# Seven block products in place of eight in the down product of a feed-forward block, each between two up tiles of the next group

## The chip, the cores and the metric

The kernel runs on one core of a Trainium2 chip. The metric is device microseconds of one execution, the median of several runs. The engines are TensorE (PE, matmuls; PEld are its weight loads), VectorE (DVE), ScalarE (ACT), GpSimd (POOL) and SyncE (SP, which here only issues DMAs).

## The reference, cut to what matters

One layer of a decoder: RMS norm, one projection, attention heads beside mLSTM heads, an output projection, and then a feed-forward block. The change touches only the last two lines of it.

```python
D_MODEL = 1024
SEQ = 512
D_FF = 4 * D_MODEL
...
    x = x + rms_norm(mixed @ w_out, g_mix_post)

    u = rms_norm(x, g_mlp_pre) @ w_up
    u = jnp.square(jax.nn.relu(u))
    x = x + rms_norm(u @ w_down, g_mlp_post)
    return x
```

Everything is float32. `u` is 512 tokens by 4096 features, `w_down` is 4096 by 1024.

## The kernel before

**Precision.** A float32 operand is split in two tiles of the matmul type fp32r: a high part (a cast, on ACT) and the rest (the operand minus the high part, on DVE). A product of two split operands is three matmuls, high by high, high by low and low by high, added up in PSUM (`three`, line 212). One matmul multiplies a stationary 128x128 block by a moving 128x512 block.

**Weights.** All weights are a list of chunks of 128x1024 floats (512 KB), in the order of their use (`specs`, from line 139). `chunk(i)` splits up to chunk i + 2 and asks for loads up to i + 4. A raw chunk goes to a ring of three buffers (tag `raw`), its split to a ring of three (tag `ws`), both in `split_to` (line 180; the cast is line 197, the subtraction line 198). The last four chunks of `w_down` go to the pool `res` instead.

**Feed-forward block.** The features come in four groups of 1024. For a group, eight up tiles `up0` to `up7` of 128 features by 512 tokens are made, each with one chunk of `w_up` as stationary blocks and the split normed input `hT` as moving operand: 8 x 3 = 24 matmuls. `up_evac` (line 833) turns one into a split operand: relu on ACT, square on DVE, cast on ACT, subtraction on DVE. Then comes the down stage: for each half of the 1024 output columns, four accumulators in PSUM (one for each 128 tokens), four chunks of `w_down`, two 128-feature rows of weights in each. A stage is 2 halves x 4 chunks x 4 token tiles x 2 x 3 = 192 matmuls. DVE adds each accumulator to `y` in SBUF (copies it for group 0; lines 908 and 910). For group 3 the second column half is kept back: it runs token tile by token tile (`dl`), each followed by the last norm, the sum with `x1` and the store.

**Order.** PE executes its instructions in the order of the program text. The order on the other engines is made by a scheduler from priorities; weight splits have a high one. Buffers of a tag are given out in turn, and a tile that takes a buffer waits for the last reader of the one before. PSUM has eight banks of 128x512 floats: four for the tag `mm` (pool `psm`), four for `at` (pool `psa`). In the second half `kts` (twelve tiles of 4 KB per partition) holds `u` of groups 1 and 3 and the four tiles of `y`; `res` holds `u` of groups 0 and 2.

Of the kernel before, what the change touches and what calls it, by code (L numbers as in the profile page):

```python
# [15 lines left out]
F32 = mybir.dt.float32  # L16
F32R = mybir.dt.float32r
# [3 lines left out]
OP = mybir.AluOpType  # L21
# [86 lines left out]
def kernel(  # L108
# [47 lines left out]
    for g in range(4):  # L156
        for m in range(8):
            up_chunks.append(len(specs))
            specs.append((w_up[g * 8 + m], 1024, "ring"))
        for half in range(2):  # L160
            for c in range(4):
                dn_chunks[g, half, c] = len(specs)
                specs.append((w_down[g, half, c], 1024, "res" if (g, half) == (3, 1) else "ring"))
    raws, splits = {}, {}
    state = {"res": None, "load": 0, "split": 0}

    def load_raw(src, n, name, parts=1):
        raw = ring.tile([P, 1024], F32, tag="raw", name=name, bufs=3)
        for a in range(parts):
            sl = slice(a * n // parts, (a + 1) * n // parts)  # L170
            nc.sync.dma_start(raw[:, sl], src[:, sl])
        return raw

    def load_to(i):
# [27 lines left out]
    def chunk(i):  # L202

        split_to(i + 2)
        load_to(i + 4)
        return splits[i]

    def mm(o, lh, rh, first, last):
        nc.tensor.matmul(o, lh, rh, start=first, stop=last)  # L209
        flow.pe(max(o.shape[-1], 256) / 2.4 + 2.5)  # L210

    def three(o, lh, ll, rh, rl, first, last):
        mm(o, lh, rh, first, False)
        mm(o, lh, rl, False, False)
        mm(o, ll, rh, False, last)

    def tr(o, i, idn):
        nc.tensor.transpose(o, i, idn)  # L218
# [553 lines left out]
    state["res"] = res  # L772

    ph2.tile([P, PAD2], F32, name="pad2")
    res.tile([P, PADR], F32, name="padr", bufs=1)
    x1, hT = [], ph2.tile([P, KT, 2, S], F32R, name="hT")
    gpo = ph2.tile([P, D], F32, name="gpo")
    gp2 = ph2.tile([P, D], F32, name="gp2")
# [5 lines left out]
    nc.sync.dma_start(gp2, g_post2.partition_broadcast(P))  # L784
# [8 lines left out]
    def second_norm(t, yB):  # L793

        r = small.tile([P, 1], F32, tag="r1", name="r1")
        tt = slice(t * P, (t + 1) * P)
        with tc.high_priority(offset=300):
            nc.scalar.activation(junk, yB, AF.Square, accum_out=s2[:, t, 1:2])
            rsqrt(r, s2[:, t, 1:2], 1.0 / D, None, "r1", extra=s2[:, t, 0:1])
            for half, y in ((0, yA[t]), (1, yB)):  # L800
                cc = slice(half * S, (half + 1) * S)
                tmp = ph2.tile([P, S], F32, tag="tmp", name="tmp", bufs=2)
                nc.vector.scalar_tensor_tensor(tmp, y, r, gpo[:, cc], op0=OP.mult, op1=OP.mult)
                nc.vector.tensor_tensor(x1[t][:, cc], tmp, x1[t][:, cc], op=OP.add)
        for half in range(2):
            yield dict(delay=DLY["norm"] if half == 0 else DLY["nrm2"])
            tp = psa.tile([P, S], F32, tag="at", name="hTp")
            for k in range(4):
                tr(tp[:, k * P:(k + 1) * P], x1[t][:, half * S + k * P:half * S + (k + 1) * P], ident)
            with tc.high_priority(offset=300):  # L810
                for k in range(4):
                    kt, src = 4 * half + k, tp[:, k * P:(k + 1) * P]
                    g = gcol[:, 8 + kt:9 + kt]
                    nc.scalar.activation(hT[:, kt, 0, tt], src, AF.Copy, scale=g)
                    nc.vector.scalar_tensor_tensor(hT[:, kt, 1, tt], src, g, f(hT[:, kt, 0, tt]), op0=OP.mult, op1=OP.subtract)  # L815
        yield dict(delay=DLY["hT"])
        flow.flags.add(f"hT{t}")
# [9 lines left out]
        flow.add(second_norm(t, yB))  # L827


    y = [None] * NT  # L830
    EARLY = 3

    def up_evac(uh, ul, ps):
        r = ph2.tile([P, S], F32, tag="ur", name="ur", bufs=2)
        nc.scalar.activation(r, ps, AF.Relu)
        nc.vector.tensor_tensor(r, r, r, op=OP.mult)  # L836
        nc.scalar.copy(uh, r)  # L837
        nc.vector.tensor_tensor(ul, r, f(uh), op=OP.subtract)  # L838

    def u_tiles(g):  # L840
        if g % 2 == 0:
            big = [res.tile([P, 2, 1024], F32R, tag="u", name=f"u{g}{i}") for i in range(4)]
            return [(big[m // 2][:, m % 2, 0:S], big[m // 2][:, m % 2, S:2 * S]) for m in range(8)]
        r = []
        for m in range(8):
            t = kts.tile([P, 2, S], F32R, tag="kt", name=f"u{g}{m}")
            r.append((t[:, 0], t[:, 1]))
        return r

    def up_ps(m):  # L850
        pool, tag = ((psm, "mm"), (psa, "at"))[m % 2]
# [11 lines left out]
    for g in range(4):  # L863
        u = u_tiles(g)
        m0 = 0
        if g == 0:
            m0 = EARLY
            wss = [chunk(up_chunks[m]) for m in range(EARLY)]
            pss = [up_ps(m) for m in range(EARLY)]
            for m in range(EARLY):  # L870
                up_mm(pss[m], wss[m], slice(0, 256))
            flow.until("hT3")
            for m in range(EARLY):
                up_mm(pss[m], wss[m], slice(256, 512))
                up_evac(u[m][0], u[m][1], pss[m])

            eps2 = ph2.tile([P, NT], F32, name="eps2")
            for t in range(NT):
                for half in range(2):
                    nc.scalar.activation(junk, x1[t][:, half * S:(half + 1) * S], AF.Square, accum_out=q2[:, t, half:half + 1])  # L880
            nc.vector.tensor_tensor(eps2, q2[:, :, 0], q2[:, :, 1], op=OP.add)
            nc.vector.tensor_scalar(eps2, eps2, 1.0 / D, EPS, op0=OP.mult, op1=OP.add)
            nc.vector.tensor_tensor(eps2, eps2, eps2, op=OP.mult)
            nc.vector.tensor_scalar(eps2, eps2, D * EPS, None, op0=OP.mult)
        for m in range(m0, 8):
            ws = chunk(up_chunks[g * 8 + m])
            ps = up_ps(m)
            up_mm(ps, ws, slice(0, S))
            up_evac(u[m][0], u[m][1], ps)
        for half in range(2):  # L890
            cc = slice(half * S, (half + 1) * S)
            if (g, half) == (3, 1):
                break
            pool, tag = ((psm, "mm"), (psa, "at"))[half]
            pd = [pool.tile([P, S], F32, tag=tag, name=f"dn{g}{half}{t}") for t in range(NT)]
            for c in range(4):
                ws = chunk(dn_chunks[g, half, c])
                for t in range(NT):
                    tt = slice(t * P, (t + 1) * P)
                    for k in range(2):  # L900
                        m, kc = 2 * c + k, slice(k * S, (k + 1) * S)
                        three(pd[t], u[m][0][:, tt], u[m][1][:, tt], ws[:, 0, kc], ws[:, 1, kc], m == 0, m == 7)
            for t in range(NT):
                if g == 0:
                    if half == 0:
                        yt = kts.tile([P, 2, S], F32R, tag="kt", name=f"y{t}")
                        y[t] = f(yt).rearrange("p a n -> p (a n)")
                    nc.vector.tensor_copy(y[t][:, cc], pd[t])
                else:
                    nc.vector.tensor_tensor(y[t][:, cc], pd[t], y[t][:, cc], op=OP.add)  # L910


    wl = [chunk(dn_chunks[3, 1, c]) for c in range(4)]
    A = slice(0, S)
    for t in range(NT):
        nc.scalar.activation(junk, y[t][:, A], AF.Square, accum_out=s2[:, t, 0:1])  # L916
        nc.vector.tensor_tensor(s2[:, t, 0:1], s2[:, t, 0:1], eps2[:, t:t + 1], op=OP.add)
        nc.gpsimd.tensor_tensor(y[t][:, A], y[t][:, A], gp2[:, A], op=OP.mult)  # L918
    for t in range(NT):
        tt = slice(t * P, (t + 1) * P)  # L920
        cuts = [(0, S)] if t < NT - 1 else [(0, 256), (256, 512)]
        for a, b in cuts:
            pd = (psa if a == 0 else psm).tile([P, S], F32, tag="at" if a == 0 else "mm", name=f"dl{t}{a}")[:, a:b]
            for m in range(8):
                c, kc = m // 2, slice((m % 2) * S + a, (m % 2) * S + b)
                three(pd, u[m][0][:, tt], u[m][1][:, tt], wl[c][:, 0, kc], wl[c][:, 1, kc], m == 0, m == 7)
# [81 lines left out]
```

## Time and profile before

| | |
|---|---|
| median of three runs | 612.13 us (611.87 to 612.18) |
| the profiled execution | 612.04 us |
| its span, first to last instruction | 610.2 us |
| mean granted TensorE clock | 0.994 |
| PE busy | 595.2 us, 98%, 2967 matmuls |
| DVE busy | 353.2 us, 58%, 735 instructions |
| ACT busy | 263.7 us, 43%, 494 instructions |
| POOL busy | 71.8 us, 12% |
| DMA | 60.79 MB, mean 100 GB/s |

The page of the profile comes from one execution. Busy times of PE overlap, since a matmul starts before the one ahead of it has left the array: the mean time of a matmul (389 ns in the feed-forward block) is longer than the time from one start to the next. So the pace is read from the length of a stretch and its number of matmuls, not from that mean. "Idle before" in the groups of instructions says what ended the idle time in front of a group. Most matmuls have one source line (L209), the line of the helper `mm`; they are told apart by the tiles they write: `up`, `dn`, `dl`.

### The profile page before, as it was taken

To read this page: it belongs to the slowest core of one execution; us is meant where nothing else is said; L and a number is where in the kernel's file an instruction comes from. 1 tells how busy PE (TensorE), PEld (TensorE's weight loads), DVE (VectorE), ACT (ScalarE), POOL (GpSimd) and SP (SyncE) were. 2 spreads that over 40 slices of the span, in tenths; PEclk is the share of its full clock that TensorE was granted. 3 is DMA by queue.
4 is the path that set the end of the run, shared out by engine and by line. 5 is a ranking of instruction groups with operands and counts; after the bars stand their busy time and mean duration, and the time that the engine had idled before them with its cause. 6 is when DMAs were issued, how large, how long until landed. Compare 5 with 4: busy or idle time off the path is not lost.

```text
span 610.2 us, 7825 instructions
## 1 busy us (share of the span) xinstructions
PE 595.2 (98%) x2967; PEld 503.4 (82%) x2967; DVE 353.2 (58%) x735; ACT 263.7 (43%) x494; POOL 71.8 (12%) x78
## 2 busy tenths in 40 slices
PE   8999998899999999999999999999999999999994
PEld 5898897789878888898888888888888888888884
DVE  5897868588987728864432444343444344445466
ACT  5654567466766734753321244312344222344311
POOL 0232431154211140000000000000000000000141
PEclk9999999899999999999999999999999999999998
DMA  7642121012311383022222222222233222233102
GB/s 283 253 143 88 62 103 36 18 45 78 104 37 68 105 304 109 1 86 88 105 103 104 86 87 103 104 104 89 84 104 104 103 95 81 102 104 112 61 35 104
DMA packets 18470, 60.79 MB, mean 100 GB/s; under 512 B 2432, under 2 KB 2432, under 8 KB 18432
## 3 DMA queue, kind: packets, MB, share of 16 engines
q1 hardware_dynamic: 18288, 60.28, 28.3%
q8 instruction: 23, 0.38, 0.3%
q14 instruction: 15, 0.12, 0.1%
q10 hardware_dynamic: 144, 0.01, 0.0%
HBM read 58.19 MB, written 2.10 MB: 99 GB/s over the span
## 4 chain that ended last, share of the span: by engine, by line
PE 81%; DVE 11%; DMA 3%; ACT 3%; issue 1%; POOL 0%; DVEq 0%; SPq 0%; ACTq 0%
PE up L209 28%; PE dn L209 25%; PE qk L209 7%; PE mo L209 4%; PE mqk L209 4%; PE gv L209 3%; PE vv L209 2%; PE ao L209 1%; PE as L209 1%; DMA raw<-in_w_up_dram 1%; ACT ws L197 1%; PE pt L218 1%; DVE r1t L302 1%; DVE ws L198 1%; PE dl L209 1%
## 5 line engine op out<-in xcount | busy, mean ns | idle before, releaser
L198 DVE TENSOR_TENSOR ws<-raw,ws 128x1024 fp32r<-128x1024 f32 (+3 forms) x85 | 102.4, 1207 | 162.5 <-ACT ws L197 162.2
L197 ACT CAST ws<-raw 128x1024 fp32r<-128x1024 f32 (+3 forms) x101 | 101.5, 1010 | 200.7 <-PE dn L209 98.4
L209 PE MATMUL up<-hT,ws 128*128 128x512 f32 (+1 forms) x840 | 177.2, 372 | 0.7 <-DVE hT L815 0.5
L209 PEld LDWEIGHTS up<-hT,ws 128*128 128x128 f32 x840 | 148.3, 188 | 28.2 <-DVE hT L815 0.6
L209 PE MATMUL dn<-ws,u 128*128 128x512 f32 x672 | 153.0, 389 | 0.0
L209 PEld LDWEIGHTS dn<-ws,u 128*128 128x128 f32 x672 | 126.2, 188 | 26.1
L198 POOL TENSOR_TENSOR ws<-raw,ws 128x1024 fp32r<-128x1024 f32 (+3 forms) x16 | 36.0, 2256 | 115.8 <-ACT ws L197 80.4
L209 PE MATMUL qk<-ws,xT 128*128 128x512 f32 x192 | 48.9, 404 | 0.0
L918 POOL TENSOR_TENSOR y<-y,gp 128x512 f32<-128x512 f32 x4 | 5.2, 1296 | 354.6 <-ACT junk L916 354.2
L209 PEld LDWEIGHTS qk<-ws,xT 128*128 128x128 f32 x192 | 36.0, 194 | 7.0
L837 ACT CAST u<-ur 128x512 fp32r<-128x512 f32 x32 | 19.9, 621 | 42.5 <-DVE ur L836 42.5
L838 DVE TENSOR_TENSOR u<-ur,u 128x512 fp32r<-128x512 f32 x32 | 22.2, 692 | 20.7 <-ACT u L837 20.7
L209 PE MATMUL mo<-ws,xT 128*128 128x512 f32 x96 | 26.0, 407 | 0.0
L209 PE MATMUL mqk<-xT,ws 128*128 128x512 f32 x96 | 23.7, 411 | 0.9 <-ACT ws L197 0.9
L209 PEld LDWEIGHTS mqk<-xT,ws 128*128 128x128 f32 x96 | 18.9, 199 | 6.2 <-ACT ws L197 1.8
L209 PE MATMUL yb<-ws,mix 128*128 128x512 f32 x96 | 23.1, 394 | 0.0
L209 PE MATMUL ya<-ws,mix 128*128 128x512 f32 x96 | 22.9, 394 | 0.0
L209 PE MATMUL dl<-ws,u 128*128 128x512 f32 (+1 forms) x120 | 22.2, 347 | 0.0
L836 DVE TENSOR_TENSOR ur<-ur 128x512 f32<-128x512 f32 x32 | 21.9, 684 | 0.0
L209 PEld LDWEIGHTS dl<-ws,u 128*128 128x128 f32 x120 | 19.4, 189 | 2.9
L678 ACT ACTIVATE pp<-as,mxs 128x128 f32<-128x128 f32 (+3 forms) x32 | 16.8, 526 | 10.5 <-DVE mxs L676 10.4
L209 PEld LDWEIGHTS ya<-ws,mix 128*128 128x128 f32 x96 | 17.7, 188 | 3.6
(261 smaller groups left out, 719.4 us busy)
## 6 DMA issues: line engine op xcount, KB each, us to landing
raw<-in_w_up_dram SPq DMA_DIRECT2D x32, 512.0 KB, 3.2
raw<-in_w_down_dram SPq DMA_DIRECT2D x32, 512.0 KB, 3.2
raw<-in_w_in_dram SPq DMA_DIRECT2D x15, 512.0 KB, 3.2
raw<-in_w_out_dram SPq DMA_DIRECT2D x8, 512.0 KB, 3.2
xs<-in_x_dram SPq DMA_DIRECT2D x4, 512.0 KB, 8.1
x<-in_x_dram SPq DMA_DIRECT2D x4, 512.0 KB, 6.7
out_dram<-y SPq DMA_DIRECT2D x8, 256.0 KB, 2.0
raw<-in_w_in_dram SPq DMA_DIRECT2D x4, 392.0 KB, 6.8
```

The costliest lines, as they stand in the source:

```text
L197: nc.scalar.copy(ws[:, 0, sl], raw[:, sl])
L198: lo.tensor_tensor(ws[:, 1, sl], raw[:, sl], f(ws[:, 0, sl]), op=OP.subtract)
L209: nc.tensor.matmul(o, lh, rh, start=first, stop=last)
L218: nc.tensor.transpose(o, i, idn)
L302: nc.vector.scalar_tensor_tensor(t, g, mh, g, op0=OP.mult, op1=OP.mult)
L678: nc.scalar.activation(po, sp[:, 0:n], AF.Exp, bias=mxs[:, i:i + 1], accum_out=rs[:, i:i + 1])
L836: nc.vector.tensor_tensor(r, r, r, op=OP.mult)
L837: nc.scalar.copy(uh, r)
L838: nc.vector.tensor_tensor(ul, r, f(uh), op=OP.subtract)
L918: nc.gpsimd.tensor_tensor(y[t][:, A], y[t][:, A], gp2[:, A], op=OP.mult)
```

## The change

In groups 0 to 2 the down product is done as a two-by-two block product with seven products in place of eight (Strassen's scheme in Winograd's form). A is `u` of the group: the first index is the token half (256 tokens), the second the feature half (512). B is the group's `w_down`: feature half by column half (512 columns). The blocks of A are `a11, a21` (tile `l`) and `a12, a22` (tile `h`), those of B the tiles `b`, two of 128x1024 for a block.

- `up_evac` now leaves the raw square in float32 in the tiles `us` (relu and square, no split).
- The blocks of `w_down` are loaded raw by `load_b` into `kts` tiles; only group 3's pass through the chunk list.
- `sums` makes the sums and differences of raw blocks that the scheme needs, in place (one of them in a `raw` buffer): four of A and eight of B tiles for a group.
- `a_split` and `b_split` split the operands of a product, 1 + 2 tiles of 128x1024. The tag `a` has two buffers, and so has `tw`.
- `p_mm` does a product: two accumulators of 128 tokens by 512 columns, 4 feature tiles, three matmuls each, 24 in all. There are three accumulator pairs for a group, X, Z and Y. X takes four products on top of each other and Y two, and after each product DVE adds the present state to a quarter of `y`. So a sum that two quarters of the output share is made in PSUM.
- The seven products of a group stand between the eight up tiles of the next group: up tile m, product m. Operands of a product are prepared one step ahead (`pre`).
- Group 3 has its down product as before, from splits made after the last up tile; half of them lie in the space of `hT`. `gpo` and the temporaries of the second norm lie in a tile `scr`, and `gp2` is loaded late. From group 1 on, all up tiles use the tag `at`.

The rows that follow are the order on PE, before, from group 0's last up tile on. `u` are splits of the group's operand, `ws` chunks of weights.

```order
L209 MATMUL up7_3204<-hT_2527,ws43_3129 128x512 x24
L209 MATMUL dn000_3234<-ws44_3164,u00_2813 128x512 x6
L209 MATMUL dn001_3235<-ws44_3164,u00_2813 128x512 x6
L209 MATMUL dn002_3236<-ws44_3164,u00_2813 128x512 x6
L209 MATMUL dn003_3237<-ws44_3164,u00_2813 128x512 x6
L209 MATMUL dn000_3234<-ws45_3199,u01_2814 128x512 x6
```

After the change, PE at the first two products of group 1 (`pX1`, `pZ1`; `w1` are splits of B, `a1` of A), which stand between up tiles of group 2.

```order
L209 MATMUL pX10_3808<-w100_3693,a10_3658 128x512 x6
L209 MATMUL pX11_3809<-w100_3693,a10_3658 128x512 x6
L209 MATMUL pX10_3808<-w101_3696,a10_3658 128x512 x6
L209 MATMUL pX11_3809<-w101_3696,a10_3658 128x512 x6
L209 MATMUL up1_3848<-hT_2526,ws53_3733 128x512 x24
L209 MATMUL pZ10_3881<-w110_3802,a11_3767 128x512 x6
L209 MATMUL pZ11_3882<-w110_3802,a11_3767 128x512 x6
```

So eight up tiles and then 32 rows of six have become up tile, four rows of six, up tile, four rows of six.

On DVE, before, the same place in a group: the end of group 1's first column half. `ur` and `u` belong to `up_evac`, `y` are the adds from PSUM.

```order
L198 TENSOR_TENSOR ws63_3807<-raw63_3742,ws63_3807 128x1024
L198 TENSOR_TENSOR ws64_3836<-raw64_3781,ws64_3836 128x1024
L198 TENSOR_TENSOR ws65_3865<-raw65_3810,ws65_3865 128x1024
L910 TENSOR_TENSOR y0_3354<-dn100_3774,y0_3354 128x512
L910 TENSOR_TENSOR y1_3356<-dn101_3775,y1_3356 128x512
L910 TENSOR_TENSOR y2_3358<-dn102_3776,y2_3358 128x512
L910 TENSOR_TENSOR y3_3360<-dn103_3777,y3_3360 128x512
```

After the change, DVE from group 1's sum `s1` to the operands of its third product (L878 are sums, L907 subtractions of a split, L848 the square of an up tile, L945 the adds from PSUM).

```order
L878 TENSOR_TENSOR s1_3836<-u10_3223,u11_3224 128x1024
L907 TENSOR_TENSOR a11_3767<-u11_3224,a11_3767 128x1024
L878 TENSOR_TENSOR u10_3223<-u10_3223 128x1024
L198 TENSOR_TENSOR ws55_3843<-raw55_3736,ws55_3843 128x1024
L848 TENSOR_TENSOR u20_3765<-u20_3765 128x2x256
L907 TENSOR_TENSOR w110_3802<-b1100_3628,w110_3802 128x1024
L945 TENSOR_TENSOR y0_3292<-pX10_3808,y0_3292 128x512
L945 TENSOR_TENSOR y1_3294<-pX11_3809,y1_3294 128x512
L907 TENSOR_TENSOR w111_3805<-b1101_3630,w111_3805 128x1024
L907 TENSOR_TENSOR a12_3840<-s1_3836,a12_3840 128x1024
L878 TENSOR_TENSOR s1_3836<-s1_3836,u10_3223 128x1024
L878 TENSOR_TENSOR u11_3224<-u11_3224,s1_3836 128x1024
```

Where one split stood for each 24 matmuls of the down stage, there are now three splits, up to three or four sums, a square, the split of an up chunk and two adds for each 48 matmuls.

On ACT, after the change, the end of the feed-forward block: the casts for group 3 stand among the casts of its chunks.

```order
L847 ACTIVATE u31_4304<-up6_4731 128x2x256
L906 CAST a31_4821<-u30_4303 128x1024
L197 CAST ws72_4890<-raw72_4835 128x1024
L197 CAST ws70_4832<-raw70_4729 128x1024
L847 ACTIVATE u31_4304<-up7_4789 128x2x256
L197 CAST ws73_4919<-raw73_4864 128x1024
L906 CAST hT_2526<-u31_4304 128x1024 x2
```

Before, a cast of 128x512 into `u` stood behind each relu there; now the last two casts are wide ones, behind the last relu and one more chunk.

The core of the diff, with the new functions:

```diff
-        for half in range(2):
-            for c in range(4):
-                dn_chunks[g, half, c] = len(specs)
-                specs.append((w_down[g, half, c], 1024, "res" if (g, half) == (3, 1) else "ring"))
+    for half in range(2):
+        for c in range(4):
+            dn_chunks[half, c] = len(specs)
+            specs.append((w_down[3, half, c], 1024, "res" if half else "ring"))
...
+    STEPS = (("X", 0, 0, (0, 0)), ("Z", 0, 0, (1, 0)), ("Y", 1, 1, (0, 0)), ("Y", 0, 1, (1, 1)),
+             ("X", 0, 1, (0, 0)), ("X", 1, 1, (0, 1)), ("X", 1, 0, (0, 0)))
...
+    def up_evac(g, m, ps):
+        d = a_tile(g, m)
+        nc.scalar.activation(d, ps.rearrange("p (h n) -> p h n", h=2), AF.Relu)
+        nc.vector.tensor_tensor(d, d, d, op=OP.mult)
...
+            t = f(kts.tile([P, 2, S], F32R, tag="kt", name=f"b{g}{r}{c}{k}")).rearrange("p a n -> p (a n)")
+            with tc.issue_after(state["dma"].ins):
+                nc.sync.dma_start(t, w_down[g, c, 2 * r + k])
...
+        if s == 2:
+            ops[g] = ring.tile([P, 1024], F32, tag="raw", name=f"s{g}", bufs=3)
+            sub(ops[g], a21, a22, op=OP.add)
+        if s == 3:
+            sub(ops[g], ops[g], a11)
+            sub(a12, a12, ops[g])
+        if s == 5:
+            sub(a21, a11, a21)
+        for k in range(2):
+            if s == 2:
+                sub(b(1, 1)[k], b(1, 2)[k], b(1, 1)[k])
+            if s == 4:
+                sub(b(1, 1)[k], b(2, 2)[k], b(1, 1)[k])
+            if s == 5:
+                sub(b(1, 2)[k], b(2, 2)[k], b(1, 2)[k])
+            if s == 6:
+                sub(b(1, 1)[k], b(2, 1)[k], b(1, 1)[k])
+
+    def two(o, src):
+
+        nc.scalar.copy(o[:, 0], src)
+        nc.vector.tensor_tensor(o[:, 1], src, f(o[:, 0]), op=OP.subtract)
...
+        src = (l[:, 0], h[:, 0], ops.get(g), h[:, 0], ops.get(g), l[:, 1], h[:, 1])[s]
+        t = res.tile([P, 2, 1024], F32R, tag="a", name=f"a{g}{s}", bufs=2)
+        two(t, src)
...
+            t = ph2.tile([P, 2, 1024], F32R, tag="tw", name=f"w{g}{s}{k}", bufs=2)
+            two(t, src[k])
...
+    def p_mm(g, s, a, w):
+        key, th, oh, _ = STEPS[s]
+        new = s < 3
+        if new:
+            acc[key] = [psm.tile([P, S], F32, tag="mm", name=f"p{key}{g}{i}") for i in range(2)]
+        for c in range(2):
+            for i in range(2):
+                for k in range(2):
+                    j, kc = 2 * c + k, slice(k * S, (k + 1) * S)
+                    ac = slice(j * 256 + i * P, j * 256 + (i + 1) * P)
+                    three(acc[key][i], a[:, 0, ac], a[:, 1, ac], w[c][:, 0, kc], w[c][:, 1, kc], new and j == 0, j == 3, not new)
...
+            if g == 0 and s in (0, 2, 3, 6):
+                nc.vector.tensor_copy(y[t][:, cc], acc[key][i])
+            else:
+                nc.vector.tensor_tensor(y[t][:, cc], acc[key][i], y[t][:, cc], op=OP.add)
...
+    for g in range(3):
+        new_group(g + 1)
+        for m in range(8):
+            n = 7 * g + m
+            if m < 7:
+                pre(n + 1, 0)
+            up_unit(g + 1, m)
+            if m == 7:
+                break
+            pre(n + 1, 1)
+            if g < 2 and m == 5:
+                load_b(g + 1, 0, 0)
+                load_b(g + 1, 1, 0)
+            if g < 2 and m == 6:
+                load_b(g + 1, 0, 1)
+                load_b(g + 1, 1, 1)
+            p_mm(*steps[n], at[n], bt[n])
...
+    for i, (th, fh) in enumerate(((0, 0), (1, 0), (0, 1), (1, 1))):
+        if fh == 0:
+            u[th, fh] = res.tile([P, 2, 1024], F32R, tag="a", name=f"a3{i}", bufs=2)
+        else:
+            u[th, fh] = hv[:, th * 2048:(th + 1) * 2048].rearrange("p (a n) -> p a n", a=2)
+        two(u[th, fh], us[3][fh][:, th])
```

More of the change, by code (lines that the diff above doesn't have):

```diff
@@ L170, in load_raw @@
             sl = slice(a * n // parts, (a + 1) * n // parts)
[L171 removed]
+            state["dma"] = nc.sync.dma_start(raw[:, sl], src[:, sl])
         return raw
@@ L801, in second_norm @@
                 cc = slice(half * S, (half + 1) * S)
-                tmp = ph2.tile([P, S], F32, tag="tmp", name="tmp", bufs=2)
+                tmp = tmps[half]
                 nc.vector.scalar_tensor_tensor(tmp, y, r, gpo[:, cc], op0=OP.mult, op1=OP.mult)
@@ L913, with new_group, load_b @@
-    wl = [chunk(dn_chunks[3, 1, c]) for c in range(4)]
+    us, bs, acc = {}, {}, {}
+    def new_group(g):
+        us[g] = [f(res.tile([P, 2, 1024], F32R, tag="u", name=f"u{g}{i}")) for i in range(2)]
+    def load_b(g, r, c):
+        b = []
+        for k in range(2):
+            t = f(kts.tile([P, 2, S], F32R, tag="kt", name=f"b{g}{r}{c}{k}")).rearrange("p a n -> p (a n)")
+            with tc.issue_after(state["dma"].ins):
+                nc.sync.dma_start(t, w_down[g, c, 2 * r + k])
+            b.append(t)
+        bs[g, r, c] = b
@@ new lines, in sub, with sums @@
+    def sub(o, a, b, op=OP.subtract):
+        nc.vector.tensor_tensor(o, a, b, op=op)
+    ops = {}
+    def sums(g, s):
+        (l, h), b = us[g], lambda r, c: bs[g, r - 1, c - 1]
+        a11, a21, a12, a22 = l[:, 0], l[:, 1], h[:, 0], h[:, 1]
+        if s == 2:
[15 more added lines that the diff above has]
+                sub(b(1, 1)[k], b(2, 1)[k], b(1, 1)[k])
@@ new lines, with pre, up_unit @@
+    steps = [(g, s) for g in range(3) for s in range(7)]
+    at, bt = {}, {}
+    def pre(n, part):
+        if n >= len(steps):
+            return
+        g, s = steps[n]
+        if part == 0:
+            sums(g, s)
+            at[n] = a_split(g, s)
+        else:
+            bt[n] = b_split(g, s)
+    def up_unit(g, m):
+        ws = chunk(up_chunks[g * 8 + m])
+        ps = up_ps(g, m)
+        up_mm(ps, ws, slice(0, S))
+        up_evac(g, m, ps)
+    flow.until("hT1")
+    new_group(0)
@@ new lines @@
+    wss = [chunk(up_chunks[m]) for m in range(EARLY)]
+    pss = [up_ps(0, m) for m in range(EARLY)]
+    for m in range(EARLY):
+        up_mm(pss[m], wss[m], slice(0, 256))
+    flow.until("hT3")
+    for m in range(EARLY):
+        up_mm(pss[m], wss[m], slice(256, 512))
+        up_evac(0, m, pss[m])
+    eps2 = ph2.tile([P, NT], F32, name="eps2")
+    for t in range(NT):
+        for half in range(2):
+            nc.scalar.activation(junk, x1[t][:, half * S:(half + 1) * S], AF.Square, accum_out=q2[:, t, half:half + 1])
@@ new lines @@
+    ph2.tile([P, PADR], F32, name="padr")
+    nc.vector.tensor_tensor(eps2, q2[:, :, 0], q2[:, :, 1], op=OP.add)
+    nc.vector.tensor_scalar(eps2, eps2, 1.0 / D, EPS, op0=OP.mult, op1=OP.add)
+    nc.vector.tensor_tensor(eps2, eps2, eps2, op=OP.mult)
+    nc.vector.tensor_scalar(eps2, eps2, D * EPS, None, op0=OP.mult)
+    for m in range(EARLY, 8):
+        if m == 4:
+            load_b(0, 0, 0)
+            load_b(0, 1, 0)
+        if m == 6:
+            load_b(0, 0, 1)
+            load_b(0, 1, 1)
+            pre(0, 0)
+        if m == 7:
+            pre(0, 1)
+        up_unit(0, m)
@@ new lines, in dn3 @@
+    def dn3(o, t, m, w, first, last):
+        a, ac = u[t // 2, m // 4], slice((m % 4) * 256 + (t % 2) * P, (m % 4) * 256 + (t % 2 + 1) * P)
+        three(o, a[:, 0, ac], a[:, 1, ac], w[0], w[1], first, last)
+    pd = [psm.tile([P, S], F32, tag="mm", name=f"dn{t}") for t in range(NT)]
+    for c in range(4):
+        ws = chunk(dn_chunks[0, c])
+        for t in range(NT):
+            for k in range(2):
+                kc = slice(k * S, (k + 1) * S)
+                dn3(pd[t], t, 2 * c + k, (ws[:, 0, kc], ws[:, 1, kc]), c + k == 0, c + k == 4)
@@ L914 @@
+    for t in range(NT):
+        nc.vector.tensor_tensor(y[t][:, 0:S], pd[t], y[t][:, 0:S], op=OP.add)
+    wl = [chunk(dn_chunks[1, c]) for c in range(4)]
     A = slice(0, S)
```

110 lines of the change are left out of this document (36 added, 74 removed).

## The prediction

> **What bounds the kernel now.** I read the span first, then who made TensorE (PE) wait, then the stretches of the second half one by one.
>
> ```profile
> core 0: 610.2 us, clock 0.994
> ```
>
> The execution took 612.04 us, so 1.8 us lie outside its span. The median of the three runs is 612.13. The view of waits, for PE over the whole span:
>
> ```profile
> PE sp L209 <- DVE dd L571: 2.6, 1, 2.6
> PE pw L240 <- DVE onec L225: 1.2, 1, 1.2
> PE mqk L209 <- ACT ws L197: 0.9, 1, 0.9
> PE pt L218 <- DVE a12kl L414: 0.8, 1, 0.8
> PE tp L218 <- DVE dd L559: 0.6, 1, 0.6
> PE up L209 <- DVE hT L815: 0.5, 1, 0.5
> PE tp L218 <- ACT ntmp L585: 0.4, 1, 0.4
> PE up L209 <- ACT hT L814: 0.2, 1, 0.2
> ```
>
> These are all of PE's waits: eight, 7.2 us together. None names a down product (dn, dl), and the only ones of an up product are for hT, before group 0 can begin. So the second half is a gapless stream of matmuls. The view of stretches gives its pace; the columns are us, then busy us and instruction count of PE, PEld, DVE, ACT, POOL, then granted clock, DMA share and GB/s. The first row is group 0's down stage, the second is group 1's up stage, the third is group 1's down stage, and the last is the first column half of group 3's.
>
> ```profile
> 297.46:340.98 43.52, 43.52 (x194) 36.05 (x193) 15.57 (x17) 9.55 (x10) 0.00 (x0) 1.00 0.28 97
> 340.98:384.50 43.52, 43.52 (x194) 36.05 (x192) 19.56 (x23) 16.22 (x22) 0.00 (x0) 1.00 0.28 97
> 384.50:428.02 43.52, 43.52 (x194) 36.05 (x193) 15.57 (x17) 9.55 (x10) 0.00 (x0) 1.00 0.28 97
> ...
> 558.58:580.34 21.76, 21.76 (x98) 18.02 (x96) 11.69 (x13) 9.02 (x13) 2.24 (x2) 1.00 0.21 72
> ```
>
> A stage has 192 matmuls of 128x512 (the counts include edge overlaps): 43.52 / 192 = **226.67 ns** each, in up and down stages alike, at full clock. DVE works 15.57 + 19.56 = 35.1 us of a group's 87.04, ACT 25.8. PE is the bound and the other engines have room.
>
> **What is removed.** Each of groups 0 to 2 loses 192 - 7 x 24 = 24 matmuls. That is 24 x 226.67 ns = 5.44 us a group, and **16.32 us** for three. Nothing is taken from the up stages, from group 3, or from the first half.
>
> The Trainium skill, "TensorE: Matmul & The Clock Gate", section "Back-to-back issue gap", gives N/2.4 + 2.5 ns for a warm matmul. That would be 215.8 ns, a saving of 15.5 us and a time of 596.5. The trace has 226.67 ns for this very instruction, so the measurement decides.
>
> **What is added, and what hides it.** Durations from the groups of instructions between 258 and 585 us:
>
> ```profile
> L198 DVE TENSOR_TENSOR ws<-raw,ws 128x1024 fp32r<-128x1024 f32 x61 | 74.6, 1225 | 149.9 <-ACT ws L197 149.9
> L197 ACT CAST ws<-raw 128x1024 fp32r<-128x1024 f32 x61 | 64.1, 1054 | 166.4 <-PE dn L209 98.4 <-PE up L209 65.6 <-DMA raw<-in_w_down_dram 2.4
> ...
> L836 DVE TENSOR_TENSOR ur<-ur 128x512 f32<-128x512 f32 x32 | 21.9, 684 | 0.0
> ...
> L835 ACT ACTIVATE ur<-up 128x512 f32<-128x512 f32 x32 | 18.9, 590 | 0.0
> L910 DVE TENSOR_TENSOR y<-dn,y 128x512 f32<-128x512 f32 x20 | 13.4, 687 | 10.0 <-PE dn L209 10.0
> ```
>
> A group now has 8 + 7 + 14 = 29 splits of 128x1024 (up weights, A operands, B operands), 12 sums of 128x1024 (4 of A, 8 of B), 8 squares and 14 adds from PSUM. The sums are all-f32, in place or into a scratch. That form is not in the trace at 1024 columns. Its nearest rows bound it: L836, the same form at 512 columns, doubled with its fixed part, gives 1.37 us; two starts of neighbours give the other end:
>
> ```profile
> 298.74 1.23 DVE L198 TENSOR_TENSOR ws<-raw,ws 128x1024 fp32r<-128x1024 f32 x1 [2.18 <-ACT ws L197]
> 299.89 0.68 DVE L836 TENSOR_TENSOR ur<-ur 128x512 f32<-128x512 f32 x1
> ```
>
> The second starts 1.15 us after the first. I take 1.225, the row of the same size. DVE per group: 41 x 1.225 + 8 x 0.684 + 14 x 0.687 = 65.3 us. ACT: 29 x 1.054 + 8 x 0.590 = 35.3 us. PE now needs 360 x 226.67 ns = 81.6 us a group. So DVE is at 80% (35.1 / 87.04 = 40% before), ACT at 43%. With 1.37 for the sums, DVE has 67.0. No average makes DVE the bound; what is left is the order within a step.
>
> A step is one up tile (5.44 us) and one product (5.44 us, two halves of 2.72, each with its own B tile). The tw tag has two buffers, so the next first B tile is cast when PE has finished the present first half, the second when it has finished the product. From release to use are 8.16 us, cast and subtraction take 1.05 + 1.23 = 2.28, so **5.9 us of slack** in each step, unless DVE is late. I walk DVE's rows through the fullest stretch, the passage from group 0's products to group 1's, where six sums stand between two products and a seventh and eighth behind the next pair of adds. Time 0 is the end of group 0's last product. DVE does w100 by -0.4, the two copies to y by 0.9, b1000's sum by 2.2, w101 by 3.4, three B sums by 7.1, the split ws54 by 8.3, the square of u11 by 9.0, the sum s1 by 10.2, a11 by 11.5, u10's sum by 12.7, ws55 by 13.9, a square by 14.6, w110 by 15.9, two adds by 17.3, w111 by 18.6, a12 by 19.9, two A sums by 22.3. Then it waits for the cast of ws56, which needs the up tile that ends at 21.76. PE meanwhile starts products at 10.88, 21.76 and 32.64. The one at 21.76 needs a11 (11.5), w110 (15.9) and, at 24.48, w111 (18.6): 5.9 us to spare at the least. The one at 32.64 needs a12 (19.9). So I charge **nothing** for all added splits and sums; with 1.37 us the eight sums add 1.2 us of lag, still inside 5.9.
>
> Accumulators: a product that goes on in X or Y must wait until DVE has read it, two adds of 0.69 us that end about 1 us behind the product, under the 5.44 us of the up tile in between. If that cover were gone, about 1 us a step.
>
> The DMA traffic keeps its bytes; B blocks come straight into the kts tiles, eight of 512 KB over two steps around the group's end.
>
> ```profile
> raw<-in_w_down_dram SPq DMA_DIRECT2D x32, 512.0 KB, 3.2
> ```
>
> The loads go out as DVE frees the old tiles, behind raw loads in SP's queue: the last when it has done w061, at about -8.6, so it lands near -5.4; the sums want them from 0.9 on. A lateness of 5 us beyond that would delay a11 from 11.5 to 16.5, wanted at 21.76. So nothing again. Group 0's first B tile heads DVE's queue before the split ws42 and waits for a load queued behind raw43; ws42 is used by up tile 6, three tiles (16.3 us) after the wait begins; two loads of 3.2 us and two splits of 2.3 us leave 5 us of that (an estimate from the rows above).
>
> **The tail.** Group 3's A is split after the last product, and its second feature half goes into hT's space once the last up tile is done. Let 0 be the end of the last product. PE does up tile 7 until 5.44, then four quarters of the first column half, starting at 5.44, 10.88, 16.32 and 21.76. a30 is split earlier, a31 by 2.3 (needed 8.16). ACT casts ws70 by 6.5, relu by 7.1, ws73 by 8.1, hT by 9.5 and 10.5; DVE finishes hT by 10.9 and 12.1. Needed: 16.32 and 19.04. If it were late, the cost would be that lateness once. From dl on everything stays:
>
> ```profile
> 580.34 22.23 PE L209 MATMUL dl<-ws,u 128*128 128x512 f32 x120
> ```
>
> From there to the span's end are 29.9 us before and after. In front, gpo and the temporary of the second norm move into the scratch tile, and gp2's load leaves the queue; the two hT waits of 0.7 us may go or double, so -0.7 to +0.7.
>
> **Sum.** 612.04 - 16.32 = 595.7 for an execution like the profiled one, with the median's 0.1 on top **595.8 us**, a span of 593.9.
>
> **Rivals.**
>
> *The products run at a slower pace.* They run beside a DVE twice as busy. The nearest rows lie in the first half, where the page's slices of 15.3 us (the fourth and fifth) show DVE at 7 and 8 tenths:
>
> ```profile
> DVE  5897868588987728864432444343444344445466
> ```
>
> ```profile
> 59.68 3.56 PE L209 MATMUL qk<-ws,xT 128*128 128x512 f32 x15
> 63.17 0.78 PE L542 MATMUL ac<-cs,ar 4*128 4x4 f32 x10
> ```
>
> 15 matmuls in 3.49 us are 232.7 ns. At that price 504 product matmuls take 3.0 us more: 598.8. Against it: 226.67 holds in up and down stages although DVE's load differs. This bounds the pace from above, 226.67 from below.
>
> *DVE falls behind in the full stretches.* Needs sums much dearer than the rows. The dearest 128x1024 subtraction in the trace is POOL's:
>
> ```profile
> L198 POOL TENSOR_TENSOR ws<-raw,ws 128x1024 fp32r<-128x1024 f32 x10 | 24.9, 2493 | 84.9 <-ACT ws L197 49.6 <-issue 23.5 <-DVE pp L680 11.8
> ```
>
> At 2.49 us the eight sums of the stretch add 10.1 us; less 5.9 of slack, 4.2 us of PE waiting a group, 12.6 in all: 608.4. It would be a different engine's price, so I hold it for unlikely.
>
> *DVE becomes the bound, and the kernel is slower.* The place is the whole chain of 41 wide operations a group. Break-even is where they fill the old 87.04 us: (87.04 - 15.1) / 41 = 1.75 us each. At 2.0 us a group takes 97.1, 10.1 more than before, 30 us in all: 642. For it speaks only that DVE has not been seen at 80% with both inputs in SBUF for long; against it 1.225 over 61 cases.
>
> *The change does not do what it says.* If the products kept 192 matmuls a group, 612. The order of PE shows four rows of 6 for a product; this is nearly excluded.
>
> **Chances.** Forecast 0.85 (its own range 595.0 to 596.9), slower pace 0.05, DVE late 0.05, DVE the bound 0.03, no change 0.02. Range 595.0 to 599.0: it takes in the pace's bound of 598.8 and leaves out the last three, 0.10. About 0.2% (1.2 us) is what a measurement here tells from no change. Faster 0.95, same 0.02, slower 0.03.
>
> **What would show it.** Right: 2967 - 72 = 2895 matmuls, no PE wait for a product's operand, 10.88 us per step, DVE near 353 + 3 x 30.2 = 444 us busy, sums near 1.2 us, 29.9 us from dl to the end. Wrong: PE waiting for w, a or an accumulator in the steps with sums, a matmul pace over 227 ns in the products, or ACT and DVE waiting for the B loads of a group's end long enough to reach PE.

## The result and the profile after

The changed kernel takes **596.04 us** (median of 4 runs, 595.0 to 596.14), against 612.15 for the kernel before in the same comparison. The ratio is 0.9714, 95% interval 0.9663 to 0.9765. One of the four runs of before in it took 617.23 us, which pulls the ratio down and widens its interval (the two medians alone are as 0.9737). A second comparison of the same two kernels, below, gives 0.9742 (0.9727 to 0.9756); one of its 17 runs of before was slow, with 1206.22 us, and is not in that ratio. The profiled execution took 595.0 us, 1.8 of them outside its span.

The page of the profile after: the span, the busy times, and DVE in 40 slices.

```profile
span 593.2 us, 7763 instructions
...
PE 578.5 (98%) x2895; PEld 489.2 (82%) x2895; DVE 433.0 (73%) x800; ACT 286.9 (48%) x505; POOL 72.1 (12%) x78
...
DVE  5897868687996845865688675987667986756456
```

2895 matmuls are the 72 fewer that the diff takes out. PE is at 98%, as before. DVE has risen from 58% to 73%, and in the second half (the last 20 digits) it swings between 4 and 9 tenths where before it showed 2 to 6 (the row of before is in the prediction). The view of waits, for PE over the whole span (us in total, times, longest):

```profile
PE sp L209 <- DVE dd L571: 2.6, 1, 2.6
PE pw L240 <- DVE onec L225: 1.2, 1, 1.2
PE pt L218 <- DVE a12kl L414: 0.8, 1, 0.8
PE tp L218 <- DVE dd L559: 0.6, 1, 0.6
PE mqk L209 <- DVE ws L198: 0.5, 1, 0.5
PE up L209 <- DVE hT L813: 0.5, 1, 0.5
PE tp L218 <- ACT ntmp L585: 0.4, 1, 0.4
PE up L209 <- ACT hT L812: 0.2, 1, 0.2
```

Eight again, and no product (pX, pY, pZ) among them: nothing that DVE does for the operands, sums and adds of the products reaches PE. The view of stretches, a row each for groups 0 and 1, seven products and eight up tiles (columns as in the prediction):

```profile
302.20:383.80 81.60, 81.60 (x361) 67.57 (x360) 61.76 (x65) 33.89 (x37) 0.00 (x0) 1.00 0.30 104
383.80:465.40 81.60, 81.60 (x361) 67.57 (x360) 61.76 (x65) 33.90 (x37) 0.00 (x0) 1.00 0.30 103
```

360 matmuls in 81.60 us are 226.67 ns each, to the digit the pace of before. Group 2 has one up tile less behind its last product: 336 matmuls in 76.16 us, the same pace. DVE is busy 61.76 of 81.60 us, 76%. PE's timeline (start, duration) shows the steps and the tail:

```profile
302.20 5.60 PE L209 MATMUL pX<-w,a 128*128 128x512 f32 x24
307.64 5.60 PE L209 MATMUL up<-hT,ws 128*128 128x512 f32 x24
...
372.92 11.04 PE L209 MATMUL up<-hT,ws 128*128 128x512 f32 x48
383.80 5.60 PE L209 MATMUL pX<-w,a 128*128 128x512 f32 x24
...
541.56 11.04 PE L209 MATMUL dn<-ws,a 128*128 128x512 f32 x48
552.44 11.04 PE L209 MATMUL dn<-ws,hT 128*128 128x512 f32 x48
563.32 2.88 PE L209 MATMUL dl<-ws,a 128*128 128x512 f32 x12
```

From 302.20 to 563.32 starts are 5.44 us apart everywhere (10.88 a step), the group's end included (two up tiles, 372.92 to 383.80). The last stage takes the late splits of group 3 (hT at 552.44) without a gap. From dl at 563.32 to the span's end are 29.9 us, as before.

### The profile page after: what moved, and what is told of

Its sections match the earlier page's. It is cut to its first block, busy times and chain, and to the rows that moved or that the text cites. A ratio compares the mean times of both kernels' runs of the same rounds, so it can differ in the third digit from the quotient of the medians.

```text
span 593.2 us, 7763 instructions
## 1 busy us (share of the span) xinstructions
PE 578.5 (98%) x2895; PEld 489.2 (82%) x2895; DVE 433.0 (73%) x800; ACT 286.9 (48%) x505; POOL 72.1 (12%) x78
## 4 chain that ended last, share of the span: by engine, by line
PE 84%; DVE 10%; ACT 2%; DMA 1%; issue 1%; SPq 0%; DVEq 0%; ACTq 0%
PE up L209 29%; PE pX L209 11%; PE qk L209 7%; PE pY L209 6%; PE mo L209 4%; PE ya L209 4%; PE dn L209 4%; PE gv L209 3%; PE pZ L209 3%; PE mqk L209 3%; PE vv L209 2%; PE yb L209 2%; PE ao L209 1%; PE as L209 1%; PE pt L218 1%; DVE r1t L302 1%
## 5 line engine op out<-in xcount | busy, mean ns | idle before, releaser
L197 ACT CAST ws<-raw 128x1024 fp32r<-128x1024 f32 (+3 forms) x77 | 76.3, 996 | 125.5 <-PE up L209 83.7
L198 DVE TENSOR_TENSOR ws<-raw,ws 128x1024 fp32r<-128x1024 f32 (+3 forms) x61 | 73.4, 1205 | 62.7 <-ACT ws L197 62.2
L906 ACT CAST w<-b 128x1024 fp32r<-128x1024 f32 x42 | 44.3, 1055 | 61.0 <-PE pX L209 25.5
L907 DVE TENSOR_TENSOR w<-b,w 128x1024 fp32r<-128x1024 f32 x42 | 51.4, 1224 | 25.3 <-ACT w L906 25.3
L209 PE MATMUL pX<-w,a 128*128 128x512 f32 x288 | 67.2, 389 | 0.0
L209 PEld LDWEIGHTS pX<-w,a 128*128 128x128 f32 x288 | 54.1, 188 | 11.2
L209 PE MATMUL pY<-w,a 128*128 128x512 f32 x144 | 33.6, 389 | 0.0
L209 PEld LDWEIGHTS pY<-w,a 128*128 128x128 f32 x144 | 27.0, 188 | 5.6
L878 DVE TENSOR_TENSOR b<-b,b 128x1024 f32<-128x1024 f32 x24 | 29.1, 1219 | 0.9 <-DMA b<-in_w_down_dram 0.7
L848 DVE TENSOR_TENSOR u<-u 128x512 f32<-128x512 f32 x32 | 21.9, 685 | 0.0
```

Of the source, the lines that this page charges most:

```text
L197: nc.scalar.copy(ws[:, 0, sl], raw[:, sl])
L198: lo.tensor_tensor(ws[:, 1, sl], raw[:, sl], f(ws[:, 0, sl]), op=OP.subtract)
L209: nc.tensor.matmul(o, lh, rh, start=first, stop=last, skip_group_check=go_on)
L848: nc.vector.tensor_tensor(d, d, d, op=OP.mult)
L878: nc.vector.tensor_tensor(o, a, b, op=op)
L906: nc.scalar.copy(o[:, 0], src)
```

## The experiments

Each edit is against the changed kernel. "ya" is the first matmul stage of the output projection. Its first 18 matmuls stand between those of the heads; the start of the other 78, one row in PE's timeline, is called the start of ya here. It splits an execution into the part that the change doesn't touch and the part that holds it.

**The same kernel again** (5 runs, no edit), beside 17 runs of before with a median of 611.98.

> The changed kernel once more, unchanged, against the kernel before in five rounds. Theory (the time is the number of matmuls times 226.67 ns, everything added is hidden): 595.8 us, ratio 0.9733 (16.32 us less), no wait of PE behind the first up tile; the start of ya in the trace lies between 207.8 and 208.6 us, so that the 0.7 us by which the profiled run of the change was ahead there is scatter of the start. Rival (the new place of gpo, of the temporaries and of gp2's load brings the 0.7 us too): 595.1 us, and ya starts at 207.8 again.

Measured: 595.79 us (593.8 to 596.52), ratio 0.9742 (0.9727 to 0.9756). The profiled one, with 593.8, is the fastest. Its PE timeline at ya, and the same row of after and then of before:

```profile
206.55 17.99 PE L209 MATMUL ya<-ws,mix 128*128 128x512 f32 x78
```

```profile
207.84 17.99 PE L209 MATMUL ya<-ws,mix 128*128 128x512 f32 x78
```

```profile
208.53 17.99 PE L209 MATMUL ya<-ws,mix 128*128 128x512 f32 x78
```

From that row to the end of the span: 591.9 - 206.55 = 385.35 us here, 593.2 - 207.84 = 385.36 in after, 610.2 - 208.53 = 401.67 in before. So the part with the change is the same in two executions to the 0.1 us in which spans are given, and shorter by **16.3 us**; what differs between these executions of one kernel lies ahead of ya, where no instruction was changed. The expectation had ya start between 207.8 and 208.6, and its rival at 207.8 again: 206.55 is outside of both.

**No sums.** The twelve sums a group are left out, and the split takes a raw block in the place of a sum.

```diff
     def sums(g, s):
+        return
...
-        src = (l[:, 0], h[:, 0], ops.get(g), h[:, 0], ops.get(g), l[:, 1], h[:, 1])[s]
+        src = (l[:, 0], h[:, 0], l[:, 1], h[:, 0], l[:, 1], l[:, 1], h[:, 1])[s]
```

> The twelve sums of blocks a group are left out (the third and fifth products take a21 in place of the scratch sum, so the output is not the reference's); splits, products and adds stay. Theory: sums are hidden, so 595.8 us as with them (within 0.3), with DVE some 36 x 1.2 = 42 us less busy (near 390). Rival (the sums cost PE something, by waits or by pace): less by what they cost; at 1.2 us a sum in the open up to 42 us less, 554.

Measured: 595.79 us (4 runs, 595.12 to 596.3), ratio 0.9738 (0.9723 to 0.9753), the same as with the sums. The page's busy row:

```profile
PE 578.1 (97%) x2895; PEld 488.4 (82%) x2895; DVE 391.7 (66%) x764; ACT 286.9 (48%) x505; POOL 71.9 (12%) x78
```

DVE has 36 instructions and 41 us less to do than in after, and the time doesn't move (the same 385.4 us from ya to the end). The sums cost nothing.

**Eight products instead of seven.** The eight plain block products of a group, each between the up tiles in the same way, from raw blocks and without sums.

```diff
-    STEPS = (("X", 0, 0, (0, 0)), ("Z", 0, 0, (1, 0)), ("Y", 1, 1, (0, 0)), ("Y", 0, 1, (1, 1)),
-             ("X", 0, 1, (0, 0)), ("X", 1, 1, (0, 1)), ("X", 1, 0, (0, 0)))
+    STEPS = [("X", th, oh, (fh, oh)) for oh in range(2) for th in range(2) for fh in range(2)]
...
-        src = (l[:, 0], h[:, 0], ops.get(g), h[:, 0], ops.get(g), l[:, 1], h[:, 1])[s]
+        src = us[g][s % 2][:, s // 2 % 2]
...
-        new = s < 3
+        new = s % 2 == 0
...
+        if new:
+            return
...
-    steps = [(g, s) for g in range(3) for s in range(7)]
+    steps = [(g, s) for g in range(3) for s in range(8)]
...
```

The parts left out take away the call of `sums` and set the loads of the B blocks one or two steps later.

> Eight plain block products a group in place of seven, in the same places between the up tiles (one behind each), with no sums and one add from PSUM for each quarter of y and group; everything else as in the changed kernel. Theory: 72 matmuls come back, 595.8 + 16.3 = 612.1 us, the time of the kernel before. Rival (part of the gain is from the interleaving, from the tail or from the front): less than 611.3 us by that part.

Measured: 612.79 us (12 runs, 611.31 to 614.5), ratio 1.0019 (1.0007 to 1.0032), with 2967 matmuls. Its ya starts at 208.65 of a span of 610.8: 402.15 us from there, 0.5 more than before. One wait of PE is new:

```profile
PE dn L209 <- DVE a L906: 0.2, 1, 0.2
```

So the order of the work, the raw loads, the scratch tile and the late splits give nothing by themselves; together they cost some 0.5 us here. The whole gain is the 72 matmuls.

**The products in one piece.** All seven products of a group run one after the other, then the eight up tiles: the cover of an up tile between two products is taken away. The splits of the next product, A and B, now stand ahead of a product in the program.

```diff
         for m in range(8):
...
-            if m < 7:
-                pre(n + 1, 0)
-            up_unit(g + 1, m)
...
+            if m < 6:
+                pre(n + 1, 0)
+                pre(n + 1, 1)
+            p_mm(*steps[n], at[n], bt[n])
+        for m in range(8):
...
+            up_unit(g + 1, m)
```

> The seven products of a group stand together behind its eight up tiles, with no up tile between them; the same instructions else. Theory (the up tile is the cover of the splits: from release of a w buffer to its use only 2.72 us are left, the cast and subtraction take 2.28, and DVE has adds and sums between; an accumulator that goes on must be read first): PE waits 1 to 3 us a product, 21 of them, 617 to 659 us, slower than the kernel before. Rival (DVE's average is what counts: about 36 us of work in a product stage of 38.1 us, so no cover is needed): 596 to 598 us.

Measured: 621.29 us (4 runs, 620.93 to 625.69), ratio 1.0172 (1.0143 to 1.0201), 9 us **slower than before** with the same 72 matmuls saved. PE's waits at products:

```profile
PE pX L209 <- DVE y L945: 10.6, 6, 3.2
PE pY L209 <- DVE y L945: 3.0, 7, 0.5
...
PE pZ L209 <- DVE a L907: 1.9, 3, 0.6
...
PE pY L209 <- DVE a L907: 1.0, 3, 0.3
PE pY L209 <- DVE y L943: 0.9, 2, 0.5
```

15 of the 21 waits are for `y`: for DVE to read an accumulator in which the next product goes on. None is for a B tile (w), which the expectation had put first. The timeline of PE at the longest of them in group 0 and in group 2:

```profile
321.33 5.81 PE L209 MATMUL pX<-w,a 128*128 128x512 f32 x24
330.34 7.06 PE L209 MATMUL pX<-w,a 128*128 128x512 f32 x24 [3.20 <-DVE y L945]
...
512.53 5.69 PE L209 MATMUL pX<-w,a 128*128 128x512 f32 x24 [3.20 <-DVE y L945]
```

The product at 321.33 has its last matmul's start 23 x 226.67 ns later, at 326.5; the next begins at 330.34. What DVE does meanwhile, in its timeline:

```profile
326.10 1.23 DVE L907 TENSOR_TENSOR w<-b,w 128x1024 fp32r<-128x1024 f32 x1
327.23 1.23 DVE L907 TENSOR_TENSOR a<-u,a 128x1024 fp32r<-128x1024 f32 x1
328.37 1.23 DVE L907 TENSOR_TENSOR w<-b,w 128x1024 fp32r<-128x1024 f32 x1
329.50 1.29 DVE L945 TENSOR_TENSOR y<-pX,y 128x512 f32<-128x512 f32 x2
```

The read stands in DVE's queue behind three splits for products to come. It is short (it starts at 329.50 and PE goes on at 330.34), but it is late. The three stages of products take 47.4, 47.7 and 46.1 us where 168 matmuls need 38.1: 27.0 us lost in all, of which the 17.4 us of the rows above are idle. The rest is in two things: a wait costs some 0.3 us more than the idle time shown (at the longest 330.34 - 326.77 = 3.57 us from where the product was due, for 3.20 shown; 21 times 0.3 are 6 us), and after the idle of 3.2 us the clock is lower for a while, in two of the three groups. The view of stretches, from the start of that product to the next one's, in group 0 and in group 2:

```profile
330.34:337.75 7.41, 7.06 (x25) 5.41 (x25) 4.69 (x6) 1.32 (x2) 0.00 (x0) 0.81 0.00 0
```

```profile
512.53:518.60 6.07, 5.69 (x25) 4.43 (x25) 4.70 (x6) 1.34 (x2) 0.00 (x0) 1.00 0.00 0
```

At a granted clock of 0.81 the same work takes 1.3 us longer. In group 1, not shown, the clock was 0.78.

**A dose of DVE work.** Two, four or eight operations of 128x512, on a tile that nothing else uses at that time, are put ahead of each product's A split.

```diff
             sums(g, s)
+            for _ in range(k):
+                sub(junk, junk, junk, op=OP.max)
             at[n] = a_split(g, s)
```

> Two more DVE operations of 128x512 (0.66 us, on a tile nobody else uses at that time) are put in front of each product's A split: 21 x 2. DVE is busy 61.8 us of a group's 81.6 in the trace of the change; this makes it 61.8 + 7 x 1.3 = 71. Theory (5.9 us of slack a step, DVE catches up in each step): no change, 595.8 us, and from the start of ya to the end of the span 385.4 us as before the dose. Rival (the full stretches are already near the edge): waits of PE at products behind the stretch with eight sums, some us.

> Four such operations a product: DVE 61.8 + 7 x 2.6 = 80 us of a group's 81.6. Theory: still under the bound on average, but the full stretch (eight sums within 33 us of PE time) now lags by more than the 5.9 us of slack: PE waits of 0 to 5 us a group, 596 to 611 us. Rival (only the average counts): 595.8 us.

> Eight such operations a product: DVE 61.8 + 7 x 5.3 = 99 us of a group's 81.6, so DVE is the bound. Theory: 17 us more a group, 3 x 17 = 52 us, 640 to 652 us, slower than the kernel before; the break-even with the kernel before lies where DVE's work fills 87 us a group. Rival (PE hides more, since up tiles do not wait for DVE): less than 630 us.

Measured, beside 3 runs of before (613.34): two, 597.01 us, ratio 0.9737 (0.9698 to 0.9777); four, 594.91, ratio 0.9703 (0.9657 to 0.9749); eight, 618.62, ratio 1.009 (1.0055 to 1.0125). Two runs each, so the first two are not told apart from after. With four, one group in the view of stretches:

```profile
302.40:384.00 81.60, 81.60 (x361) 67.57 (x360) 81.05 (x97) 34.21 (x38) 0.00 (x0) 1.00 0.30 104
```

DVE is busy 81.05 of 81.60 us and PE still loses nothing in the products (from ya to the end it is 0.2 us more than in after, and those lie ahead of group 0). Here the expectation of up to 5 us of waiting a group was wrong: with this dose DVE's total counted, not where its work lies in a step. With eight, in the same view, groups 0 and 1:

```profile
302.64:384.24 81.60, 81.60 (x361) 67.57 (x360) 81.34 (x101) 33.91 (x37) 0.00 (x0) 1.00 0.31 104
384.24:475.71 91.47, 83.72 (x362) 68.61 (x360) 91.17 (x116) 33.81 (x37) 0.00 (x0) 0.96 0.28 92
```

The first group still runs free while DVE falls behind; from then on DVE sets the time. Again the wait is the read of an accumulator (PE's timeline):

```profile
446.82 7.29 PE L209 MATMUL pX<-w,a 128*128 128x512 f32 x24 [7.38 <-DVE y L945]
```

The expectation for eight was 21 to 33 us too high. Two things were left out of it that account for most of this: the group in which the lag builds up, which cost nothing, and that neighbours on DVE overlap. An extra operation shows 0.68 us, but the next instruction starts 0.60 us after it; a wide one shows 1.22, and the next starts 1.14 after it.

**One B buffer.** The tag `tw` gets one buffer, so that no split of B can be made ahead.

```diff
-            t = ph2.tile([P, 2, 1024], F32R, tag="tw", name=f"w{g}{s}{k}", bufs=2)
+            t = ph2.tile([P, 2, 1024], F32R, tag="tw", name=f"w{g}{s}{k}", bufs=1)
```

> One buffer in place of two for the splits of B (tag tw), all else as in the changed kernel. Theory: the second B tile of a product can be cast only when PE has read the first, so PE stands for cast and subtraction (1.05 + 1.23 us, with semaphores 2.3 to 2.5) in the middle of each of 21 products; the first tile of the next product is still covered by the up tile: 595.8 + 48 to 53 = 644 to 649 us. If the waits drop the granted clock, more. Rival (something else than this chain sets when a product can go on): far less than 40 us more.

Measured: 654.6 us (2 runs, 654.22 and 654.97), ratio 1.0677 (1.0637 to 1.0716). PE's timeline, a product of group 0 and the up tile behind it, and then the second half of a later product:

```profile
301.74 2.88 PE L209 MATMUL pX<-w,a 128*128 128x512 f32 x12
305.76 0.50 PE L209 MATMUL pX<-w,a 128*128 128x512 f32 x1 [1.13 <-ACT w L906]
307.02 2.79 PE L209 MATMUL pX<-w,a 128*128 128x512 f32 x11 [0.76 <-DVE w L907]
309.64 5.60 PE L209 MATMUL up<-hT,ws 128*128 128x512 f32 x24
...
373.68 4.33 PE L209 MATMUL pX<-w,a 128*128 128x512 f32 x11 [0.76 <-DVE w L907]
```

A product takes 309.64 - 301.74 = 7.90 us instead of 5.44. The 2.46 us more are about the cast and the subtraction of the second B tile (1.05 and 1.22 us), now in the open. That is 51.7 us for 21 products, within the 48 to 53 worked out beforehand; what the measured time has beyond that is the clock. In 5 of the 21 products the last 11 matmuls take some 1.56 us longer (4.33 against 2.79), 7.8 us together. The view of stretches for the second half of two neighbours:

```profile
360.35:362.84 2.49, 2.49 (x11) 2.09 (x12) 1.90 (x2) 0.00 (x0) 0.00 (x0) 1.00 0.08 15
373.68:377.73 4.05, 4.05 (x11) 3.23 (x12) 0.69 (x1) 0.00 (x0) 0.00 (x0) 0.59 0.41 129
```

**The kernel before, twice**, to see how far two comparisons of one kernel with itself lie apart, and where.

> The kernel before once more, to see its scatter. Theory (the first microseconds, with the first loads and the first matmuls, differ from execution to execution, and the change has no part in it): ya starts anywhere between 206.5 and 208.9 us, as in the traces of the changed kernel; from there to the end of the span 401.7 us as in the first trace, which is 16.3 more than the changed kernel's 385.4. Rival (the change moves the front): ya starts at 208.5 again, and later than in the mean of the changed kernel's traces (207.9).

> The same as e6_before_a, a second trace: scatter of the start of ya between 206.5 and 208.9 us, 401.7 us from there to the end (theory); 208.5 again (rival).

Measured beside 15 runs with a median of 611.8: 611.24 (8 runs, 610.37 to 612.73), ratio 0.9979 (0.9959 to 0.9998), and 611.89 (8 runs, 610.38 to 613.24), ratio 1.0009 (0.9994 to 1.0024). The kernel doesn't differ from itself, and yet the first interval just leaves out 1, so 0.2% is indeed about what a comparison here can tell. In the timeline of PE ya starts at 207.08 in the first and 208.12 in the second, spans 608.8 and 609.8: 401.7 us from there in both, as in the first execution of before. What differs between two executions of one kernel lies ahead of ya here too. Over the traced executions ya starts at 207.9 us in the mean of three of before and at 207.9 in the mean of nine of after and its variants, so the change itself moves nothing ahead of ya.

## Why the prediction was right, and where it failed

**The bound and the size: right.** "PE is the bound", 72 matmuls at 226.67 ns, 16.32 us. Measured between ya and the end: 401.7 - 385.4 = 16.3. Eight products in the same order give the old time within 0.5 us, so no other part of the change has a share in the gain. The median came out 0.2 us above the 595.8 of the sum. The pace in the products is 226.67 ns too: the rival of a slower pace falls. The 215.8 ns that the prediction worked out from the Trainium skill, "TensorE: Matmul & The Clock Gate", section "Back-to-back issue gap", are not what this stream shows; the page gives that formula for a single matmul apart from a stream.

**The failing step: the front, and with it the low end of the range.** The prediction allowed for the front that "the two hT waits of 0.7 us may go or double, so -0.7 to +0.7" and put the low end at 595.0. The hT waits did stay (0.5 and 0.2 us). All else ahead of the change was taken as the same in every execution, and it isn't: over nine executions of after and of its variants ya starts between 206.55 (the same kernel again) and 208.89 (two extra DVE operations), a scatter of 2.3 us; over three of before between 207.08 and 208.53. The traces show two sources. One is the first projection (mqk), whose waits for its first weights are up to 1.6 us long and in varying places; the twelve traced executions reach the wait named next up to 1.15 us apart (its end lies between 107.92 and 109.07). The other is one of the eight waits that the prediction lists, `sp` for `dd`, 2.6 us long in every execution: behind it the granted clock falls in some executions and not in others. Here are PE's timeline at the wait and the view of stretches over the fourteen matmuls behind it (two of `sp`, twelve of qk), for before and then for the same kernel in the first of its two repetitions:

```profile
108.77 0.47 PE L209 MATMUL sp<-m1q,m3k 128*128 128x128 f32 x1 [2.58 <-DVE dd L571]
...
108.77:113.26 4.49, 4.49 (x15) 3.71 (x15) 3.62 (x6) 2.89 (x3) 0.52 (x1) 0.66 0.00 0
```

```profile
108.70 0.33 PE L209 MATMUL sp<-m1q,m3k 128*128 128x128 f32 x1 [2.58 <-DVE dd L571]
...
108.70:111.78 3.08, 3.08 (x14) 2.58 (x15) 2.76 (x6) 2.58 (x3) 0.52 (x1) 1.00 0.00 0
```

The same work takes 1.4 us longer at 0.66. Of the twelve traced executions eight show a clock of 0.66 to 0.70 over the 5 us behind this wait, and their ya starts at 207.84 or later; four show 1.00 (the same kernel again, one piece, one B buffer, the first repetition of before), and there it starts at 207.39 or earlier. That is the larger part of why the same kernel again took only 593.8 us in its profiled execution. The profiled execution of before had the low one, and so, by their mean clock of 0.994 or 0.995 in place of 0.997, had eight of the nine runs of the changed kernel without an edit: that the median agrees with the sum to 0.2 us is luck to this extent, with 1.4 us at stake. A front term of -2 to +1, read from several executions, would have put the low end near 593.8.

This scatter alone doesn't take a median out of the range, and both medians (596.04 and 595.79) lie within it. The first comparison's ratio, 0.9714, times the 612.13 from which the prediction started is 594.6, below the low end, and it is so low because of the one run of before with 617.23 us: without it the same three runs give 0.9734, or 595.9. No trace of that run was kept, so where its 5 us lie stays open. The prediction had no term for such a run, while its upper end had 3 us for costs. Why the first weights come at varying times is open too.

**DVE: right in kind, the term a little too large.** Forecast 65.3 us a group, measured 61.76 (over the whole execution 444 and 433.0). The sums were not the error: the row of the B sums gives 1.219 us against 1.225 taken.

```profile
L878 DVE TENSOR_TENSOR b<-b,b 128x1024 f32<-128x1024 f32 x24 | 29.1, 1219 | 0.9 <-DMA b<-in_w_down_dram 0.7
```

The sum added mean durations, and neighbours overlap by some 0.08 us. The walk through the fullest stretch held: the timeline of DVE, where group 0's last product ends at 372.92,

```profile
376.10 3.61 DVE L878 TENSOR_TENSOR b<-b,b 128x1024 f32<-128x1024 f32 x3
...
382.65 1.22 DVE L907 TENSOR_TENSOR a<-u,a 128x1024 fp32r<-128x1024 f32 x1
...
390.57 1.22 DVE L907 TENSOR_TENSOR w<-b,w 128x1024 fp32r<-128x1024 f32 x1 [0.30 <-ACT w L906]
...
394.23 1.23 DVE L878 TENSOR_TENSOR u<-u,s 128x1024 f32<-128x1024 f32 x1
```

gives 6.8 us for the three B sums (forecast 7.1), 10.95 for a11 (11.5), 18.9 for w111 (18.6) and 22.5 for the last A sum (22.3).

**"DVE falls behind" and "DVE becomes the bound": the first was priced too high.** It charged PE for each microsecond beyond 5.9 of slack in one stretch. Four extra operations a product, 17 us a group, filled DVE to 99% and cost nothing. Up to there DVE's total decides, and some 17 of its 19.8 free microseconds a group are shown to be usable. Beyond, the kernel does become slower than before (eight operations: 1.009), so that rival was a real mechanism with the wrong place: the wait shows first at an accumulator, not at a split of B.

**"Accumulators ... if that cover were gone, about 1 us a step": too low.** In one piece it costs 27 us over 21 products, 1.3 us each on average but up to 3.6 us in one (326.77 to 330.34), because the read queues behind splits that DVE does ahead; behind that wait the clock fell in two groups of three. Whether reads put ahead of those splits would save the products in one piece was not tried. The second w buffer, which the prediction named as the source of the slack, is worth 51.7 us plus the clock.

**The tail and the loads: right.** dn, dl and the 29.9 us behind them show no wait; the B loads hold DVE up for 0.7 us in all, in the row above, and PE never.

## What to carry to other kernels

When PE runs gapless, a scheme that removes matmuls is worth its matmuls at the measured pace, if the added operands and reads of accumulators stand beside other matmuls; the same seven products in one piece lost to eight. Judge an in-order engine by its total in a stretch, from the starts of neighbours and not from mean durations, and look for the short read that queues behind long work. Take the scatter of the parts that a change doesn't touch from several executions before giving a range, and look at the clock behind every wait of PE, in the parts that stay too.

## What was not expected of the hardware

The granted clock fell behind short idle times of PE, and not each time. One of 2.58 us in the first half gave 0.66 to 0.70 over the next 5 us in eight executions and 1.00 in four. An idle of 3.2 us gave 0.81 and 0.78 over the next product in two groups and 1.00 in the third. Two idles of 1.1 and 0.8 us, 0.5 us of work between them, were followed by a slow half product in 5 of 21 products (granted 0.59 over 4 us in the one shown) and not in the other 16 (1.00 in its neighbour). The Trainium skill, "TensorE: Matmul & The Clock Gate", section "What's actually happening", has the clock halved after an idle window of some 3.4 us that runs free of the kernel. That the outcome varies from one execution or product to the next agrees with a window running free; that 2.58 us, or 1.1 + 0.8 us, of idling was enough doesn't fit one that must be idle throughout, and the measurement decides. The price was 1.3 to 1.6 us behind these waits, and 1.7 and 2.5 behind the two idles of 7.4 us with eight operations (7.13 and 7.97 us for a product in place of 5.44).

No version that beats both kernels came out of the runs. The DVE time that is left, some 17 us a group, might carry another such step; that was not tried, and group 3 has no up tiles behind it to cover its products.
